# A block sum of the weights made by an accumulating DMA, for seven block pairs a layer

## The chip, the core and the metric

The kernel runs on one core of one Trainium2 chip. TensorE multiplies, VectorE (DVE) and ScalarE (ACT) work on tiles, GpSimd (POOL) does next to nothing here, and SyncE (SP) issues nearly all DMAs. The metric is the device time of one execution in microseconds; the time before is the median of three runs.

## What is computed

A decoder trunk of two layers over 512 tokens of width 1024, all in float32:

```python
def hybrid_layer(x, g_mix, w_in, sinks, w_a, w_b, w_out, g_mlp, w_up, w_down):
    h = rmsnorm(x, g_mix)
    z = h @ w_in
    ...
    ya = sliding_window_sink_attention(aq, ak, av, sinks) @ w_a
    ...
    yb = r.astype(x.dtype) @ w_b
    mixed = jax.nn.sigmoid(ga) * ya + jax.nn.sigmoid(gb) * yb
    x = x + mixed @ w_out
    h2 = rmsnorm(x, g_mlp)
    x = x + jnp.square(jax.nn.relu(h2 @ w_up)) @ w_down
    return x
```

`r` is the retention branch with its norm and gate. The change concerns the weights `w_b` (1024 by 1024), `w_out` (1024 by 1024) and `w_up` (1024 by 4096).

## The kernel before

The weights are laid out in units of 128 x 1024 numbers (512 KB) and come in the order that `unit_order` (line 58) writes down: 168 units a layer. A unit goes through three steps: a DMA loads it into a raw tile (`load_until`, line 185; three raw tiles of the pool `wpool`), ScalarE rounds it to a high part (line 255) and VectorE subtracts that from it to get the low part (line 256); then TensorE multiplies. Each product of float32 numbers is three matmuls (`products`, lines 301 to 303): high by high, high by low, low by high. There are three tiles for high and three for low parts, so the split of a unit waits until TensorE is done with the unit three before it. `split_until` (line 231) is called three units ahead of the multiplication and calls `load_until` for two more.

Some output chunks are computed two at a time as a *pair*: a 2 by 2 block product by Winograd's form of Strassen's scheme, with seven block products in place of eight. A layer has 19 pairs: for `w_b` the chunks 0 and 2, for `w_out` 2, 4 and 6, for `w_up` 4, 6 and from there each even chunk up to 30. A pair's four parts are units of their own. With `one` and `two` for the two weight rows of blocks, each with a left and a right block of 128 x 512:

- part 0: left is `one`'s left block, right is the sum of `two`'s blocks (line 221, VectorE)
- part 1: left is that sum minus `one`'s left (line 224), right is `one`'s right block
- part 2: left is `one`'s left minus `two`'s right (line 228), right is a difference out of part 1 (line 229)
- part 3: `two`'s left block

`load_part` (line 205) loads for part 0 the left block of `one` (line 210) and the whole of `two` (line 212, a raw tile of its own), and for part 1 the right block of `one` (line 215, into a tile of another pool). `add_part` (line 217) makes the sums just before the splits. `narrow_pair` (line 584) multiplies the pairs of `w_b`, `w_out` and chunk 4 of `w_up` with 256-wide matmuls; `wide_pair` (line 1250) multiplies the others with one 512-wide and one 256-wide matmul for each block (lines 1259 and 1260). Between the parts ScalarE and VectorE evacuate (lines 595 to 611 and 1286 to 1312).

Around these pairs both vector engines also have the norm's sums (lines 312, 391 to 395), the sums of input blocks for the pairs (lines 559 to 564) and the gates (lines 858, 1134, 1148), and SyncE reloads `x` (line 1181) and the gates put aside (lines 1107, 1119).

The text's order is not the order of the engines: the kernel is built with `schedule_with_timeline_sim=True` (line 1557), and a planner with durations of its own decides which of the ready instructions an engine's queue gets next. On the chip each queue then runs in that order and an instruction that has to wait holds up all behind it.

POOL has 14 instructions: constants and masks at the start, a memset in each layer's attention (line 646, the second one at 685 us) and one scaling at the end (line 531).

Of the kernel before, what the change touches and what calls it, by code (L numbers as in the profile page):

```python
# [14 lines left out]
ALU = mybir.AluOpType  # L15
# [42 lines left out]
def unit_order():  # L58

    def plain(name, *at):  # L60
        return [(name, i) for i in range(*at)]

    def pairs(src, *firsts):
        return [("pair", j, part, src) for j in firsts for part in range(4)]

    order = plain("w_in", 26) + plain("w_a", 4) + plain("w_in", 26, 46)
    order += pairs("w_b", 0, 2) + plain("w_b", 4, 8)
    order += plain("w_out", 2) + pairs("w_out", 2, 4, 6)
    for what, q, i in mlp_sequence():
        if what == "first":  # L70
            order += plain("w_up", 4)
        elif what == "pair":
            order += pairs("w_up", 8 * q + 2 * i)
        elif what == "down":
            order += plain("w_down", 8 * q + 2 * i, 8 * q + 2 * i + 2)
        else:
            order += plain("w_down", 8 * q, 8 * q + 8)
    return order
# [48 lines left out]
def decoder(ctx, tc, xT, x_first, w_in, w_a, w_b, w_out, w_up, w_down, tables, decay, band, triangles, g_last, out):  # L127
    nc = tc.nc
# [16 lines left out]
    def big(name, dtype=F32):  # L145
        return tmp.tile([P, 2, T], dtype, tag="big", name=name, bufs=7)
# [18 lines left out]
    order = [(layer, *u) for layer in range(DEPTH) for u in unit_order()]  # L165
    raws, parts, homes = {}, {}, []
# [8 lines left out]
    def raw_tile():  # L175
        return wpool.tile([P, UNIT], F32, tag="raw", name="raw")
# [8 lines left out]
    def load_until(n):  # L185
        while state["loaded"] < min(n, len(order)):
            i = state["loaded"]
            layer, name, j = order[i][:3]
            if name == "pair":
                load_part(i)  # L190
            else:
                raws[i] = raw_tile()
                for at in halves(i):
                    queue = nc.scalar if i == 0 and at.start == 0 else nc.sync
                    queue.dma_start(raws[i][:, at], weights[name][layer, j][:, at])
                    if i < 3:
                        load_x()
            state["loaded"] += 1
# [3 lines left out]

    LEFT, RIGHT = slice(0, UNIT // 2), slice(UNIT // 2, UNIT)

    def load_part(i):
        layer, _, j, part, src = order[i]
        one, two = (weights[src][layer, j + a] for a in range(2))
        if part == 0:
            raws[i] = raw_tile()
            nc.sync.dma_start(raws[i][:, LEFT], one[:, LEFT])  # L210
            raws[i + 3] = raw_tile()
            nc.sync.dma_start(raws[i + 3], two)
        elif part == 1:
            raws[i] = big("raw2").rearrange("p a t -> p (a t)")
            nc.sync.dma_start(raws[i][:, RIGHT], one[:, RIGHT])

    def add_part(i):
        part = order[i][3]
        if part == 0:
            w2 = raws[i + 3]  # L220
            nc.vector.tensor_tensor(raws[i][:, RIGHT], w2[:, RIGHT], w2[:, LEFT], ALU.add)  # L221
        elif part == 1:
            w1 = raws[i - 1]
            nc.vector.tensor_tensor(raws[i][:, LEFT], w1[:, RIGHT], w1[:, LEFT], ALU.subtract)
        elif part == 2:
            raws[i] = big("raw3").rearrange("p a t -> p (a t)")
            w1, w2, z2 = raws[i - 2], raws[i + 1], raws[i - 1]
            nc.vector.tensor_tensor(raws[i][:, LEFT], w1[:, LEFT], w2[:, RIGHT], ALU.subtract)
            nc.vector.tensor_tensor(raws[i][:, RIGHT], z2[:, RIGHT], z2[:, LEFT], ALU.subtract)

    def split_until(n):
        while state["split"] < min(n, len(order)):
            i = state["split"]
            load_until(i + 3)
            paired = order[i][1] == "pair"
            if paired:
                add_part(i)
            raw = raws[i]
            if homes and i >= len(order) - len(homes):
                home = homes[len(order) - 1 - i]  # L240
                hi, lo = (home[:, 2 * a : 2 * a + 2, :].rearrange("p a t -> p (a t)") for a in range(2))
            else:


                first = (ASIDE, ASIDE) if paired else (0, 0)
                if paired and order[i][4] == "w_up" and wide(order[i][2]):
                    first = (ASIDE, 0)
                hi, lo = (
                    wpool.tile([P, UNIT + P], F32R, tag=n, name=n)[:, a : a + UNIT] for n, a in zip(("hi", "lo"), first)
                )  # L250
            for at in (LEFT,) if paired and order[i][3] == 3 else halves(i):
                if i == 0 and at.start == 0:
                    nc.vector.tensor_copy(hi[:, at], raw[:, at])
                else:
                    nc.scalar.activation(hi[:, at], raw[:, at], AF.Copy)  # L255
                last_low[:] = [nc.vector.tensor_tensor(lo[:, at], raw[:, at], f32(hi[:, at]), ALU.subtract).ins]  # L256
            raws.pop(i - 3 if paired else i, None)
            parts[i] = (hi, lo)
            state["split"] += 1
# [1302 lines left out]
```

## Time and profile before

| | |
|---|---|
| median of three runs | 1479.97 us (1479.74 to 1479.98) |
| the profiled execution's own time | 1481.1 us |
| its span | 1478.5 us |
| units' high parts, line 255 (ScalarE) | 334 of 1.00 us mean |
| units' low parts, line 256 (VectorE) | 335 of 1.15 us mean |
| block sums of the pairs, line 221 (VectorE) | 38 of 0.69 us median |
| DMA traffic | 166.13 MB, 112 GB/s over the span |

The profile is of one execution. A matmul's duration in it is that of the whole pipeline, so that matmuls overlap: what one costs is read from the starts of two that follow each other. A row of the order of time gives start, duration, engine, line, operation, the tile written and the tiles read, shapes and, in brackets, how long the engine was idle before it and what ended that. A row that ends in "x2" stands for two. DMA issues on SyncE's queue are marked SPq.

### The profile page before, as it was taken

The numbers are of one execution on the slowest core, as the hardware profiler recorded it, in microseconds if no ns is written. First come the engines' busy times: TensorE is split into PE (matmuls) and PEld (weight loads), VectorE is DVE, ScalarE is ACT, GpSimd is POOL, SyncE is SP. The second block draws the span as 40 slices with busy tenths as digits, with TensorE's granted clock in tenths as the row PEclk, the third lists the DMA queues.
The fourth block names the chain that finished last, engine by engine and source line by source line (L and its number), as shares of the span: only waits on it lengthen the run. The fifth ranks groups of instructions, "written<-read, shape, count | busy, mean of one in ns | idle before, by whom it ended". The sixth has DMA issues, their size and how long they took to land.

```text
span 1478.5 us, 20008 instructions
## 1 busy us (share of the span) xinstructions
PE 1467.9 (99%) x7466; PEld 1249.9 (85%) x7466; DVE 1162.7 (79%) x1920; ACT 810.3 (55%) x1302; POOL 3.8 (0%) x14
## 2 busy tenths in 40 slices
PE   9999999999999999999999999999999999999998
PEld 7888888888988888888888888888889888888887
DVE  7998668778998787776678975686889977878763
ACT  7656356654674445444556743656547654444553
POOL 0000000000000000000000000000000000000000
PEclk9999999999999999999999999999999999999999
DMA  6422223246323333333543232323553323333241
GB/s 226 135 87 86 93 82 104 93 164 191 102 79 114 100 114 94 106 100 115 170 128 91 85 98 89 99 92 98 175 167 104 101 97 99 115 101 112 89 141 57
DMA packets 56945, 166.13 MB, mean 112 GB/s; under 512 B 6896, under 2 KB 7056, under 8 KB 56848
## 3 DMA queue, kind: packets, MB, share of 16 engines
q1 hardware_dynamic: 56560, 164.33, 34.9%
q8 instruction: 58, 0.95, 0.3%
q10 hardware_dynamic: 288, 0.52, 0.1%
q14 instruction: 39, 0.32, 0.1%
HBM read 153.80 MB, written 8.40 MB: 110 GB/s over the span
## 4 chain that ended last, share of the span: by engine, by line
PE 86%; DVE 6%; issue 6%; DMA 1%; ACT 0%; POOLq 0%; DVEq 0%; SPq 0%
PE mm L303 20%; PE mm L301 20%; PE mm L302 20%; PE mm L1259 10%; PE mm L1260 5%; DVE lo L256 2%; PE rv L301 2%; PE rv L302 2%; PE rv L303 2%; DVE r L309 1%; PE score L797 1%; PE r L301 1%; PE r L303 1%; PE r L302 1%; DMA inv<-row 0%
## 5 line engine op out<-in xcount | busy, mean ns | idle before, releaser
L302 PE MATMUL mm<-r,hi 128*128 128x512 f32 (+1 forms) x1568 | 572.7, 367 | 0.0
L301 PE MATMUL mm<-r,hi 128*128 128x512 f32 (+1 forms) x1568 | 570.6, 368 | 1.4 <-ACT eu L598 0.7
L303 PE MATMUL mm<-r,lo 128*128 128x512 f32 (+1 forms) x1568 | 563.1, 367 | 1.6 <-DVE lo L256 1.3
L255 ACT ACTIVATE hi<-raw 128x1024 fp32r<-128x1024 f32 (+1 forms) x334 | 334.4, 1003 | 393.1 <-PE mm L302 210.9
L256 DVE TENSOR_TENSOR lo<-raw,hi 128x512 fp32r<-128x512 f32 (+1 forms) x335 | 385.2, 1152 | 118.8 <-ACT hi L255 115.7
L303 PEld LDWEIGHTS mm<-r,lo 128*128 128x128 f32 x1568 | 293.3, 188 | 51.1 <-DVE lo L256 3.7
L301 PEld LDWEIGHTS mm<-r,hi 128*128 128x128 f32 x1568 | 294.0, 188 | 50.2 <-ACT eu L598 1.5
L302 PEld LDWEIGHTS mm<-r,hi 128*128 128x128 f32 x1568 | 294.3, 188 | 45.7
L1259 PE MATMUL mm<-r,hi 128*128 128x512 f32 x728 | 251.9, 391 | 0.0
L1260 PE MATMUL mm<-r,lo 128*128 128x256 f32 x728 | 200.4, 277 | 1.2 <-DVE lo L256 1.1
L1259 PEld LDWEIGHTS mm<-r,hi 128*128 128x128 f32 x728 | 136.5, 188 | 28.3
L1260 PEld LDWEIGHTS mm<-r,lo 128*128 128x128 f32 x728 | 136.6, 188 | 5.2 <-DVE lo L256 2.7
L1339 DVE TENSOR_TENSOR x<-x,mm 128x512 f32<-128x512 f32 x56 | 37.8, 687 | 29.2 <-PE mm L303 29.2
L1332 ACT ACTIVATE z<-z 128x512 f32<-128x512 f32 x56 | 32.5, 624 | 48.3 <-DVE z L1312 48.3
L302 PE MATMUL rv<-lo,r 128*128 128x512 f32 x128 | 49.8, 389 | 0.0
L303 PE MATMUL rv<-hi,r 128*128 128x512 f32 x128 | 49.5, 389 | 0.0
L301 PE MATMUL rv<-hi,r 128*128 128x512 f32 x128 | 49.4, 390 | 0.0
L308 ACT ACTIVATE r<-z 128x512 fp32r<-128x512 f32 x64 | 38.7, 621 | 12.6 <-DVE z L1022 12.5
L309 DVE TENSOR_TENSOR r<-z,r 128x512 fp32r<-128x512 f32 x64 | 43.1, 686 | 2.8 <-ACT r L308 2.6
L824 ACT ACTIVATE sm<-sm,st 128x256 f32<-128x256 f32 (+1 forms) x64 | 30.2, 474 | 19.1 <-DVE st L812 18.9
L1312 DVE SCALAR_TENSOR_TENSOR z<-z,rstd 128x512 f32<-128x512 f32 x52 | 35.7, 687 | 0.6
L221 DVE TENSOR_TENSOR raw<-raw 128x512 f32<-128x512 f32 x38 | 26.0, 684 | 7.0 <-DMA raw<-w_up_in 6.3
(261 smaller groups left out, 1693.0 us busy)
## 6 DMA issues: line engine op xcount, KB each, us to landing
raw<-w_in_in SPq DMA_DIRECT2D x89, 512.0 KB, 3.6
raw<-w_down_in SPq DMA_DIRECT2D x64, 512.0 KB, 3.6
raw<-w_up_in SPq DMA_DIRECT2D x36, 512.0 KB, 3.6
raw<-w_up_in SPq DMA_DIRECT2D x56, 256.0 KB, 2.8
raw<-w_b_in SPq DMA_DIRECT2D x12, 512.0 KB, 4.0
raw<-w_out_in SPq DMA_DIRECT2D x10, 512.0 KB, 7.1
raw<-w_a_in SPq DMA_DIRECT2D x8, 512.0 KB, 3.5
aside<-gb SPq DMA_DIRECT2D x8, 512.0 KB, 4.7
```

Source lines behind the costliest of these rows:

```text
L255: nc.scalar.activation(hi[:, at], raw[:, at], AF.Copy)
L256: last_low[:] = [nc.vector.tensor_tensor(lo[:, at], raw[:, at], f32(hi[:, at]), ALU.subtract).ins]
L301: nc.tensor.matmul(ps, ah, bh, start=start and i == 0, stop=False, **more)
L302: nc.tensor.matmul(ps, ah, bl, start=False, stop=False, **more)
L303: nc.tensor.matmul(ps, al, bh, start=False, stop=stop and i == n - 1, **more)
L308: nc.scalar.activation(hi, src, AF.Copy)
L309: nc.vector.tensor_tensor(lo, src, f32(hi), ALU.subtract)
L1259: nc.tensor.matmul(both, hi[:, c], m, start=start and k == 0, stop=False, **more)
L1260: nc.tensor.matmul(ps[:, :H], lo[:, c], m[:, 0, :], start=False, stop=k == 3 and start, **more)
L1312: nc.vector.scalar_tensor_tensor(z[:, :, at], z[:, :, at], 0.0, factor, ALU.max, ALU.mult)
L1332: nc.scalar.activation(z[:, i, :], z[:, i, :], AF.Square)
L1339: nc.vector.tensor_tensor(x[:, c, :], x[:, c, :], ps, ALU.add)
```

## The change

For a pair that is `summed`, that is all pairs of `w_b` and `w_out` and the chunks 4 and 6 of `w_up` (seven a layer, 14 in all), VectorE's sum at line 221 is left out. In its place SyncE loads `two`'s right block a second time, straight into the right half of part 0's tile, and a DMA issued by POOL adds `two`'s left block from HBM onto it. The other twelve pairs a layer stay as they were. `two` is still loaded whole, since parts 2 and 3 need it.

```diff
+    def summed(i):
+
+        _, _, j, _, src = order[i]
+        return src != "w_up" or j < 8
+
     def load_part(i):
...
             raws[i + 3] = raw_tile()
             nc.sync.dma_start(raws[i + 3], two)
+            if summed(i):
+                nc.sync.dma_start(raws[i][:, RIGHT], two[:, RIGHT])
+                nc.gpsimd.dma_start(raws[i][:, RIGHT], two[:, LEFT], accum_op=ALU.add)
         elif part == 1:
...
         if part == 0:
             w2 = raws[i + 3]
+            if summed(i):
+                return
             nc.vector.tensor_tensor(raws[i][:, RIGHT], w2[:, RIGHT], w2[:, LEFT], ALU.add)
```

## The prediction, made before the changed kernel ran

> **What bounds the kernel now.** I read the page first, then the busy time by stretches around the pairs that change, then TensorE's waits, then the order of time at each of these waits.
>
> ```profile
> span 1478.5 us, 20008 instructions
> PE 1467.9 (99%) x7466; PEld 1249.9 (85%) x7466; DVE 1162.7 (79%) x1920; ACT 810.3 (55%) x1302; POOL 3.8 (0%) x14
> ```
>
> TensorE is busy all but 10.6 us of the span. Whatever the change does for VectorE, it can earn only what TensorE now loses to waits, and only near the seven pairs. In the first layer these lie between 295 and 450 us:
>
> ```profile
> 345.00:360.00 15.00, 15.00 (x68) 12.43 (x67) 15.00 (x19) 7.62 (x10) 0.00 (x0) 1.00 0.74 244
> 360.00:390.00 30.00, 29.63 (x200) 27.17 (x200) 29.19 (x44) 17.67 (x27) 0.00 (x0) 1.00 0.30 91
> 390.00:410.00 20.00, 19.33 (x136) 17.85 (x136) 19.34 (x32) 14.57 (x23) 0.00 (x0) 1.00 0.39 129
> 410.00:430.00 20.00, 20.00 (x107) 17.27 (x106) 19.41 (x21) 13.41 (x17) 0.00 (x0) 1.00 0.25 79
> 460.00:600.00 140.00, 140.00 (x707) 119.02 (x706) 110.35 (x169) 67.75 (x101) 0.00 (x0) 1.00 0.33 103
> ```
>
> The columns are the stretch, its length, and the busy time of PE, PEld, DVE, ACT and POOL, then PE's clock, the DMA share and GB/s. From 345 to 430 us VectorE is busy 82.94 of 85 us: here it is a second bound beside TensorE, unlike in the long middle part (110 of 140). The clock is 1.00 everywhere. TensorE's waits of the whole kernel are few:
>
> ```profile
> PE mm L303 <- DVE lo L256: 1.3, 2, 0.7
> PE mm L1260 <- DVE lo L256: 1.1, 3, 0.5
> ...
> PE mm L301 <- ACT eu L598: 0.7, 2, 0.4
> PE mm L301 <- ACT eu L602: 0.5, 2, 0.3
> ```
>
> Apart from the warm-up's, left out here, all of them are waits for the low part of a split weight (line 256) or for an evacuation, and in each layer they stand at the pairs. This list undercounts, as a matmul's modelled end reaches over the next one's start; I therefore measure a loss from start to start. The next rows show the largest two of the first layer and the third.
>
> ```profile
> 388.29 1.06 ACT L255 ACTIVATE hi<-raw 128x1024 fp32r<-128x1024 f32 x1
> 386.24 0.69 DVE L221 TENSOR_TENSOR raw<-raw 128x512 f32<-128x512 f32 x1
> 386.84 0.74 DVE L312 SCALAR_TENSOR_TENSOR r<-x,r 128x512 fp32r<-128x512 f32 x1
> ...
> 390.91 1.22 DVE L256 TENSOR_TENSOR lo<-raw,hi 128x1024 fp32r<-128x1024 f32 x1
> 391.12 0.28 PE L301 MATMUL mm<-r,hi 128*128 128x256 f32 x1
> 391.23 0.28 PE L302 MATMUL mm<-r,hi 128*128 128x256 f32 x1
> 392.18 0.38 PE L303 MATMUL mm<-r,lo 128*128 128x256 f32 x1 [0.67 <-DVE lo L256]
> 428.87 0.63 DVE L221 TENSOR_TENSOR raw<-raw 128x512 f32<-128x512 f32 x1
> 433.88 1.22 DVE L256 TENSOR_TENSOR lo<-raw,hi 128x1024 fp32r<-128x1024 f32 x1
> 434.29 0.40 PE L1259 MATMUL mm<-r,hi 128*128 128x512 f32 x1
> 435.16 0.38 PE L1260 MATMUL mm<-r,lo 128*128 128x256 f32 x1 [0.47 <-DVE lo L256]
> 337.62 0.40 PE L302 MATMUL mm<-r,hi 128*128 128x512 f32 x1
> 338.10 0.50 PE L303 MATMUL mm<-r,lo 128*128 128x512 f32 x1
> ```
>
> A 256-wide matmul follows the one before it after 0.12 us (391.12 to 391.23). At 392.18 there lie 0.95 us between two starts, so 0.83 are lost. A 512-wide one takes twice the pitch, 0.23: at 435.16 there lie 0.87, so 0.64 are lost; at 338.10 it is 0.48, so 0.25.
>
> **The change, part by part.** *Removed:* 14 of the 38 adds of line 221, seven a layer. An add lasts 0.69 but the next instruction starts after 0.60 (386.24 to 386.84), so each frees 0.60 us of VectorE, 8.4 us in all. Most of that is not worth anything, because VectorE catches up with a late input somewhere and then waits. It counts where VectorE runs through, without idling, from an add to a split that TensorE waits for. The add at 386.24 leads to the split at 390.91 that way (the rows of that chain have no idle time behind them), so TensorE gets back 0.60 of its 0.83. The add at 428.87 leads to the split at 433.88: 0.60 of 0.64. For the first projection's second pair the following rows count:
>
> ```profile
> 325.39 0.69 DVE L221 TENSOR_TENSOR raw<-raw 128x512 f32<-128x512 f32 x1
> 326.24 1.06 ACT L255 ACTIVATE hi<-raw 128x1024 fp32r<-128x1024 f32 x1 [1.51 <-DVE raw L221]
> ```
>
> ScalarE's split idled 1.51 us for this add, and VectorE runs from there to 338; it gives the 0.25 at 338.10. So one layer earns 0.60 + 0.60 + 0.25 = 1.45. The waits listed above come in equal pairs for the two layers (two waits on line 303 of at most 0.7, together 1.3), so two layers earn 2.9. The other four adds of a layer I cost at nothing: after them VectorE waits for another engine before the next split that TensorE waits for, as in these two rows:
>
> ```profile
> 381.24 0.42 DVE L608 TENSOR_TENSOR z<-mm,eu 128x256 f32<-128x256 f32 x1 [0.38 <-PE mm L303]
> 425.60 3.36 DVE L432 RECIPROCAL rstd<-rstd 128x512 f32<-128x512 f32 x1 [0.59 <-ACT rstd L431]
> ```
>
> If I am wrong there, the two waits on ScalarE's evacuations are what could shrink (1.2 us in the list).
>
> *Added on SyncE's queue:* 14 plain loads of 256 KB, `two`'s right block straight into the sum's place. *Added on POOL's queue:* 14 accumulating loads of 256 KB. In all 7.3 MB on top of 166.13, and the question is only whether the sum has landed when ScalarE splits it.
>
> ```profile
> 304.85 0.38 SPq L210 DMA_DIRECT2D raw<-w_b_in  x1
> 318.10 0.41 SPq L215 DMA_DIRECT2D raw<-w_b_in  x1
> 321.42 0.33 SPq L212 DMA_DIRECT2D raw<-w_b_in  x1
> 349.57 0.34 SPq L210 DMA_DIRECT2D raw<-w_out_in  x1
> 376.92 0.33 SPq L210 DMA_DIRECT2D raw<-w_out_in  x1
> raw<-w_b_in SPq DMA_DIRECT2D x8, 256.0 KB, 2.6
> raw<-w_out_in SPq DMA_DIRECT2D x12, 256.0 KB, 7.3
> 360.99 1.06 ACT L255 ACTIVATE hi<-raw 128x1024 fp32r<-128x1024 f32 x1 [2.88 <-PE mm L302]
> 363.01 1.22 DVE L256 TENSOR_TENSOR lo<-raw,hi 128x1024 fp32r<-128x1024 f32 x1
> 370.86 0.28 PE L301 MATMUL mm<-r,hi 128*128 128x256 f32 x1
> ```
>
> The first three rows are one pair: its left block (line 210) is issued at 304.85, and `two` (line 212) only at 321.42, when a slot comes free. Line 215, which stands behind line 212 in the text, went ahead of it at 318.10. So the planner doesn't hold a load behind one that waits for a slot, and the new right-block load, which goes into the same tile as the left block, should go out right behind line 210, 0.4 us later. POOL's queue holds nothing else in these stretches, so what stands behind the accumulate's wait for its own load is the next accumulate alone.
>
> The trace has no accumulating DMA and none issued by POOL. From below its price is one plain load at a quiet time, 2.6 us; from above, a read and a write-back that both pass the crowded queues, twice 7.3, so 14.6 us. I take two quiet loads in series, 5.2, because outside the stretch at 345 to 360 the DMA share is 0.25 to 0.39. The time there is: from 376.92 to 388.29, 11.4 us, against 0.4 + 2.6 + 5.2 = 8.2, so the sum is 3 us early. For the pair issued at 349.57 the queues are crowded (share 0.74): 0.4 + 7.3 + 5.2 = 12.9 against 11.4 up to the split at 360.99, 1.5 us late. That split's low part ends at 364.23 and the first 256-wide matmul of the output projection comes at 370.86, so 6.6 us cover it; without this cover it would cost 1.5 a layer. Behind the late split ScalarE holds the splits of the gated sums, which have the same cover. For the pair of 304.85 the sum no longer waits for `two` at all: 21.4 us are there before 326.24, so ScalarE's 1.51 of idling goes.
>
> [...]
>
> [...]
>
> *Sum:* 1478.5 - 2.9 = 1475.6 for the span. The median of the runs, 1479.97, lies 1.5 above the span, so 1477.1 us.
>
> **Rivals.**
>
> *The sum comes late.* If the new load is issued behind line 212 after all, as it stands in the text, the pair of 321.42 has 326.24 - 321.42 = 4.8 us, against 0.4 + 2.6 + 5.2 = 8.2: 3.4 late. VectorE's low part follows ScalarE's without a gap, and TensorE runs up to it within a few tenths, so about 3 us are lost a layer there, 6 in all; the other pairs have some cover. Of the 2.9 the last 0.25 of each layer falls away, 2.4 remain: 1479.97 + 6 - 2.4 = 1483.6. It decides from a landing 4.8 us after `two` is issued. The same follows, with the load issued early, if an accumulate takes over 8.4 us (11.4 less 0.4 and 2.6). For it: the trace has no price for an accumulate. Against: the order at 318.10.
>
> [...]
>
> *Nothing moves.* The planner lays out all queues anew, and a freed 0.60 can go into another wait: TensorE stands still for the next evacuation instead. 1479.97 within 0.5 us. For it: VectorE idles nearly nowhere from 345 on, so its order is decided by due times as much as by length.
>
> *More is freed.* With the sum there early, ScalarE's splits move forward too and all waits of the list but the warm-up's vanish, counted from start to start: besides the 2.9 the rest at 392.18 (0.23) and 435.16 (0.04) and the two waits on evacuations, 1.2 in the list; with the modelled overlap of some 0.15 each about 2 us more in two layers, 1475.1 and, with the short pauses that no list shows, down to 1473.
>
> **How the numbers follow.** Forecast 0.42, late sum 0.17, port 0.06, nothing moves 0.17, more freed 0.18. What a measurement of this kernel can tell from no change is about 0.2%, 3.0 us, so the bound to faster is 1477.0 and the forecast lies on it: half of it counts as faster (0.22), half as the same (0.20). Faster is 0.22 + 0.18 = 0.40; the same 0.20 + 0.15 = 0.35; slower 0.17 + 0.06 + 0.02 = 0.25. The likeliest case's own range is 1475.3 to 1479.0. The range of all reaches from 1473.0 over the port and most of the late sums to 1485.5, as an accumulate near its upper bound costs more than the 3.4 counted.
>
> **What would show it.** Right: line 221 has 24 instructions; the new SyncE loads stand right behind line 210; ScalarE's splits of these pairs wait for no DMA; the starts at 338, 392 and 435 us and at their places in the second layer are 0.25, 0.60 and 0.60 closer to the matmul before. Wrong: ScalarE or VectorE idle at a first part of a pair with a DMA as releaser; adds beside POOL's DMAs longer than 0.69; or TensorE's total of waits stays, with other names in it.

## The result, and the profile after

The changed kernel takes 1495.38 us (median of four runs, 1494.7 to 1499.23) against 1479.89 for the kernel before on the same chip: the ratio is 1.011, with a 95% interval of 1.0093 to 1.0128. It is slower by 15.5 us, where 1477.1 was forecast; the range ended at 1485.5.

In `load_part` line 210 (`one`'s left block) has become 215, 212 (`two`) is 217 and 215 (`one`'s right block) is 223. The functions from `add_part` on stand ten lines lower: line 221 has become 231, 224 is 234, 255 and 256 are 265 and 266, 301 to 303 are 311 to 313, 598 is 608, 1259 and 1260 are 1269 and 1270. New are SyncE's load (line 219) and POOL's accumulating DMA (line 220). The head of the page of the changed kernel:

```profile
span 1493.5 us, 20063 instructions
PE 1471.5 (99%) x7466; PEld 1253.6 (84%) x7466; DVE 1154.3 (77%) x1906; ACT 809.5 (54%) x1302; POOL 16.0 (1%) x28
```

VectorE has lost its 14 adds (1920 to 1906 instructions, 8.4 us less of busy time), as the change says. TensorE's idle time is 1493.5 - 1471.5 = 22.0 us, before it was 10.6; the other 3.6 of the 15.0 us by which the span grew are busy time of TensorE, which does the same 7466 matmuls. Its four largest waits in the whole kernel, with total, count and longest:

```profile
PE mm L311 <- ACT eu L608: 6.3, 4, 2.5
PE mm L1270 <- DVE lo L266: 3.5, 2, 1.9
PE mm L311 <- ACT rstd L441: 2.7, 2, 1.3
PE mm L311 <- ACT eu L612: 1.7, 2, 0.8
```

The same two kinds stand first as before, an evacuation by ScalarE and VectorE's low part, but several times as long; the wait for the norm's square root (line 441) is new. No DMA stands in TensorE's list, so one goes a step back, to what held VectorE and ScalarE. The view of line 220's instructions says who waited for the sums, and when they landed, counted from the start of POOL's issue:

```profile
L220 POOL DMA_DIRECT2D raw<-w_out_in x6: 853/862/872, 359.1 to 1123.0; - x6
...
  DVE raw L234: 20.1, 9
  ACT hi L265: 11.2, 2
...
DMA to landing us min/median/max: 4.0/5.2/6.4
```

Line 234 is the surprise. It is part 1's subtraction, "that sum minus `one`'s left", so it reads the sum as well, and VectorE stood still for it for 20.1 us in nine places. One of them, in the order of time, on SyncE's queue, POOL, VectorE, ScalarE and TensorE (some rows left out):

```profile
379.90 0.33 SPq L215 DMA_DIRECT2D raw<-w_out_in  x1
380.28 0.42 SPq L219 DMA_DIRECT2D raw<-w_out_in  x1
384.44 0.86 POOL L220 DMA_DIRECT2D raw<-w_out_in  x1 [16.67 <-DVE z L618]
```

```profile
384.45 0.68 DVE L239 TENSOR_TENSOR raw<-raw 128x512 f32<-128x512 f32 x1
385.66 1.22 DVE L266 TENSOR_TENSOR lo<-raw,hi 128x1024 fp32r<-128x1024 f32 x1
390.27 0.69 DVE L234 TENSOR_TENSOR raw<-raw 128x512 f32<-128x512 f32 x1 [3.40 <-DMA raw<-w_out_in]
390.88 0.41 DVE L1209 TENSOR_TENSOR x<-x,mm 128x256 f32<-128x256 f32 x1
```

```profile
391.33 0.72 ACT L321 ACTIVATE r<-x 128x512 fp32r<-128x512 f32 x1 [2.84 <-DVE x L1209]
392.48 0.36 ACT L608 ACTIVATE eu<-mm 128x256 f32<-128x256 f32 x1
393.00 1.05 ACT L265 ACTIVATE hi<-raw 128x1024 fp32r<-128x1024 f32 x1
```

```profile
390.15 0.28 PE L313 MATMUL mm<-r,lo 128*128 128x256 f32 x1
392.89 0.58 PE L311 MATMUL mm<-r,hi 128*128 128x256 f32 x1 [2.46 <-ACT eu L608]
393.27 0.41 PE L312 MATMUL mm<-r,hi 128*128 128x256 f32 x1
393.48 0.41 PE L311 MATMUL mm<-r,hi 128*128 128x256 f32 x1
```

Read it from the end. TensorE stops from 390.15 to 392.89 for an evacuation (line 608). ScalarE could not do that one, since work ahead of it on its queue waited 2.84 us for an update of `x` (line 1209). VectorE had not made the update, as the subtraction of line 234 stood ahead of it and waited 3.40 us. The subtraction waited for the accumulate, which POOL issued at 384.44; it landed 5.8 us later. POOL's row names line 618 as what it waited for, but that one had ended at 383.93. The load of 380.28 landed after 3.5 us, and at each of the four places where the view has the load's landing, POOL's issue follows it by 0.5 to 0.7 us; so the load is the likelier releaser. ScalarE's own split of the sum comes only at 393.00, without any wait for a DMA. Its queue had been held up by VectorE's stop itself, so this row doesn't tell whether the sum was in time for ScalarE; the third experiment does.

In the trace of before the subtraction stood further back, as line 224:

```profile
384.52 0.41 DVE L1199 TENSOR_TENSOR x<-x,mm 128x256 f32<-128x256 f32 x1
...
388.71 0.69 DVE L224 TENSOR_TENSOR raw<-raw 128x512 f32<-128x512 f32 x1
```

Between these two came a low part, the add of 386.24, lines 312 and 395 and another low part. The planner has taken the subtraction to the front of them, directly behind a low part of the pair before: ahead of line 1199 (now 1209) and of the four that are left when the add is gone.

The matmuls after the stop are 0.21 us apart (393.27 to 393.48) and not 0.12. The stretches around it, with the granted clock behind the five busy times:

```profile
389.00:392.50 3.50, 1.43 (x13) 1.22 (x11) 2.23 (x5) 1.17 (x3) 0.00 (x0) 1.00 0.09 16
392.50:396.00 3.50, 3.11 (x14) 3.11 (x15) 3.50 (x7) 1.56 (x4) 0.00 (x0) 0.53 0.14 37
396.00:400.00 4.00, 4.00 (x36) 4.00 (x34) 4.00 (x7) 1.43 (x2) 0.00 (x0) 0.98 0.49 152
```

For about 3.4 us the clock is at half (0.53 in the middle row, which has a little of full clock in it; in slices of half a us it is 0.74, then 0.50 from 393.0 to 396.0, then 0.85): some 1.7 us of work more are lost. One other such stretch lies in the second layer, from 1181 us on (0.50 from 1181.5 to 1184.5), also behind a stop of over 2 us. Together that is 3.4 us, nearly all of the 3.6 by which TensorE's busy time grew. In the trace of before there is no such stretch between 10 and 1470 us: the granted clock is 1.00 there in every 20 us, where the two that hold the half clock here have 0.91.

By the starts of the same matmuls, after minus before, the shift grows from 0.8 at the first pair of `w_b` to 5.2 at the third of `w_out` and 7.3 at the first matmul of `w_down`, and the second layer does the same again, to 14.7. The first 0.8 is there from the span's first 10 us on (the same matmul starts at 9.24 and at 8.46) and has nothing to do with the pairs; all the rest arises at the pairs that changed.

### The profile page after: what moved, and what is told of

Same layout as the page of the kernel before. It is cut to its first block, busy times and chain, and to the rows that moved or that the text cites. A ratio compares the mean times of both kernels' runs of the same rounds, so it can differ in the third digit from the quotient of the medians.

```text
span 1493.5 us, 20063 instructions
## 1 busy us (share of the span) xinstructions
PE 1471.5 (99%) x7466; PEld 1253.6 (84%) x7466; DVE 1154.3 (77%) x1906; ACT 809.5 (54%) x1302; POOL 16.0 (1%) x28
## 3 DMA queue, kind: packets, MB, share of 16 engines
q0 software_dynamic: 2016, 3.67, 1.6%
## 5 line engine op out<-in xcount | busy, mean ns | idle before, releaser
L234 DVE TENSOR_TENSOR raw<-raw 128x512 f32<-128x512 f32 x38 | 26.1, 688 | 20.2 <-DMA raw<-w_out_in 12.1
```

## The experiments

Four explanations were to be told apart: that the sums land late (called A in the expectations; A1 is that it acts through VectorE's subtraction, A2 through the split); that the order which the planner made anew costs by itself (B); that the new DMAs, or POOL's issuing of them, disturb the others (C); and later, that the relief is there but given back at the norm's square root (D; E is that the relief is worth nothing). All but POOL's adds at the end are edits of the changed kernel. Each was run beside the kernel before, whose median lay between 1479.73 and 1480.03.

**No accumulating DMA** (the sum then lacks `two`'s left block).

```diff
-                nc.gpsimd.dma_start(raws[i][:, RIGHT], two[:, LEFT], accum_op=ALU.add)
+                pass
```

> The accumulating DMA is left out, so that the sum is the second row's right block alone; VectorE's add stays away and SyncE's extra load stays. Theory A (the sum lands later than the planner's order allows, and VectorE and ScalarE stand in front of it): with the accumulate gone no VectorE or ScalarE instruction waits for a part-0 tile any more, and the time falls back to 1476 to 1481 us. Theory B (the order that the planner lays out without the add is bad in itself, whatever the landing): 1488 us or more. Theory C (3.67 MB more of plain loads crowd the queues): half of the loss stays, 1485 to 1490.

Measured: 1479.2 us, ratio 0.9995 (0.9986 to 1.0005). So the whole loss hangs on the accumulate; the second load from SyncE and the missing adds cost nothing together. But they also earn next to nothing: the 0.8 us by which this kernel is ahead can't be told from none by the interval. TensorE's waits in this kernel:

```profile
PE mm L311 <- ACT rstd L441: 2.7, 2, 1.3
PE mm L311 <- ACT eu L612: 1.6, 2, 0.8
...
PE mm L1270 <- DVE lo L266: 0.4, 2, 0.2
```

The waits for low parts that the forecast counted on (2.4 in all) are down to 0.4, as they should be. In their place stand new ones, at line 612 (0.5 before, now 1.6) and at the norm's square root (none before, now 2.7). Here is the latter in the order of time, on ScalarE and TensorE:

```profile
424.30 1.06 ACT L265 ACTIVATE hi<-raw 128x1024 fp32r<-128x1024 f32 x1 [3.67 <-PE mm L312]
425.38 1.28 ACT L441 ACT_TABLE_LOAD   x1
426.68 0.69 ACT L441 ACTIVATE rstd<-ssq,x 128x512 f32<-128x512 f32 x1
```

```profile
427.42 0.39 PE L311 MATMUL mm<-r,hi 128*128 128x256 f32 x1 [1.33 <-ACT rstd L441]
```

The split at 424.30 is part 2's of `w_up`'s chunk 4. In the trace of before it stood behind the square root:

```profile
424.88 0.69 ACT L431 ACTIVATE rstd<-ssq,x 128x512 f32<-128x512 f32 x1 [1.35 <-PE ssq L430]
```

Now the planner takes the split first. It waits 3.67 us for TensorE, the table load of 1.28 us comes only behind it, and the square root starts at 426.68, 1.8 us later than before. TensorE's start is 1.5 us ahead of before at the first matmul of `w_up`'s chunk 4 (0.4 of it since the first 10 us), and by the first of chunk 6 it is 0.3 behind: 1.8 are lost in between. The relief itself is there. By TensorE's starts 0.2 us are gained at 338, 0.6 at 378 and 0.9 at 392; some 0.75 are lost at 325, behind the evacuation of line 612.

**A plain DMA by POOL in the place of the accumulating one** (the sum is then a plain copy).

```diff
-                nc.gpsimd.dma_start(raws[i][:, RIGHT], two[:, LEFT], accum_op=ALU.add)
+                nc.gpsimd.dma_start(raws[i][:, RIGHT], two[:, LEFT])
```

> POOL's DMA only copies the left block over the right one, it does not add; the order of all engines is that of the changed kernel. Theory A, if what is late is the chain of two loads and POOL's issue: landing about 5 us after POOL's issue as with the add (5.2 us there), and 1493 to 1497 us. If the adding itself is what takes long (reading the destination): landing at 3 us or less, and 1480 to 1488 us.

Measured: 1482.54 us, ratio 1.0018 (1.0008 to 1.0027). All engines' orders of instructions are the same as in the changed kernel: the planner makes no difference between an accumulating DMA and a plain one. The chip does. The view of line 220's instructions:

```profile
L220 POOL DMA_DIRECT2D raw<-w_out_in x6: 536/537/538, 358.3 to 1114.8; - x6
...
  ACT hi L265: 9.5, 2
  DVE raw L234: 8.7, 7
...
DMA to landing us min/median/max: 2.9/3.7/5.3
```

The sum lands 1.5 us earlier after the start of POOL's issue (3.7 against 5.2); 0.33 of that is the issue itself (0.54 against 0.86). VectorE's waits fall from 20.1 to 8.7, and the time by 12.8 us. So with the same order, queues and traffic from HBM, the accumulate's own length is worth 12.8 of the 15.5 us, give or take some 2: this kernel's ten runs reach from 1480.7 to 1485.61. At the place shown above VectorE waits 0.78 instead of 3.40, and there is no stretch of half clock (mean granted clock 0.999, against 0.997 in the changed kernel):

```profile
385.52 0.69 DVE L234 TENSOR_TENSOR raw<-raw 128x512 f32<-128x512 f32 x1 [0.78 <-DMA raw<-w_out_in]
```

**Part 1's subtraction doesn't read the sum** (its result is then zero); the accumulates stay.

```diff
-            nc.vector.tensor_tensor(raws[i][:, LEFT], w1[:, RIGHT], w1[:, LEFT], ALU.subtract)
+            nc.vector.tensor_tensor(raws[i][:, LEFT], w1[:, LEFT] if summed(i) else w1[:, RIGHT], w1[:, LEFT], ALU.subtract)
```

> Line 234 of a summed pair subtracts the left block from itself, so that it no longer reads the sum; the accumulates stay, and only the split (ScalarE, line 265) waits for them. Theory A1 (VectorE's wait at line 234 is what costs): no VectorE wait for a part-0 DMA, ScalarE's 11 us in two places stay, and 1480 to 1485 us. Theory A2 (the wait only moves: the split's high part and with it VectorE's low part stand there in its place): 1489 us or more.

Measured: 1482.5 us, ratio 1.0017 (1.0008 to 1.0027); 12.9 us of the changed kernel's time are gone, though the sums land as late as there (5.2 us median). The waits of ScalarE for the sum stay:

```profile
ACT hi L265 <- DMA raw<-w_out_in: 11.9, 2, 6.1
```

At the place shown above the split, with nothing in its way, comes at 390.56 and doesn't wait for the accumulate, which POOL issued at 384.78 and which landed 5.3 us later, at 390.1:

```profile
390.56 1.05 ACT L265 ACTIVATE hi<-raw 128x1024 fp32r<-128x1024 f32 x1
```

So there the sum was in time for ScalarE, by half a us, and late for VectorE. TensorE's remaining waits are on evacuations and the square root:

```profile
PE mm L311 <- ACT eu L608: 2.7, 3, 1.2
PE mm L311 <- ACT rstd L441: 2.7, 2, 1.3
PE mm L311 <- ACT eu L612: 1.7, 2, 0.8
```

This tells the readers apart: 11.9 us of ScalarE's idling at the first pairs of `w_out` cost little, and nearly all of the loss goes with the 20.1 us of VectorE's. It also speaks against a disturbance by the DMAs or by POOL, since all of them are still there. What it can't tell is which of the other waits make the 3.3 us by which it and the plain copy stand above the kernel without a second step. The planner's order around the subtraction differs a little too.

**The subtraction held later**, behind the low part of part 0.

```diff
-            nc.vector.tensor_tensor(raws[i][:, LEFT], w1[:, RIGHT], w1[:, LEFT], ALU.subtract)
+            with tc.issue_after(last_low[0]) if summed(i) else ExitStack(): nc.vector.tensor_tensor(raws[i][:, LEFT], w1[:, RIGHT], w1[:, LEFT], ALU.subtract)
```

> Line 234's subtraction of a summed pair is put behind the low part of part 0 on VectorE. Theory A: VectorE's waits for DMAs at line 234 (20.1 us in 9 places) go; the late split of the output projection's first pair (ScalarE, 11.2 us in two places) stays, with its cover: 1480 to 1486 us. Theory B: the rest of the order is as new as before, 1490 us or more.

Measured: 1486.05 us, ratio 1.0041 (1.0026 to 1.0056), a hair above the range that was expected. VectorE doesn't wait for the sum any more, and 9.3 us come back, but now it is ScalarE that waits for the subtraction, as its queue shows:

```profile
389.40 1.06 ACT L265 ACTIVATE hi<-raw 128x1024 fp32r<-128x1024 f32 x1
392.70 1.06 ACT L265 ACTIVATE hi<-raw 128x1024 fp32r<-128x1024 f32 x1 [2.24 <-DVE raw L234]
```

The hold is too late here. Between the early place and this one there may be a better one; none was tried.

**A later landing**: POOL copies the block plainly first and accumulates after it (the sum is then twice the left block).

```diff
-                nc.gpsimd.dma_start(raws[i][:, RIGHT], two[:, LEFT], accum_op=ALU.add)
+                for more in ({}, dict(accum_op=ALU.add)): nc.gpsimd.dma_start(raws[i][:, RIGHT], two[:, LEFT], **more)
```

> POOL first copies the left block and then adds it, so that every sum lands about 4 us later (3.7 from issue to landing, with the plain copy). Theory A: each of the fourteen pairs now costs about what it is late, and more where TensorE pauses so long that the clock is halved: 1515 to 1550 us. Theory B (the order): 1493 to 1500 us.

Measured: 1507.13 us, ratio 1.0186 (1.0171 to 1.0202), 11.8 above the changed kernel and below the range expected for A and above the one for B. By the view of line 220's instructions ScalarE waits 28.3 us for the sums and VectorE 26.1, which is only 6.0 more than in the changed kernel. The planner knows of the extra DMA, though not of its length, and puts the subtraction later; so a third step isn't paid in full, and the kernel isn't the clean doubling it was meant to be. There are four stretches of half clock here (mean granted clock 0.995).

**One kind of pair at a time.** Three kernels, each with one line changed: only `w_b`, only `w_out`, only `w_up`'s chunks 4 and 6.

```diff
-        return src != "w_up" or j < 8
+        return src == "w_b"
```

> Only the four pairs of w_b are summed by the DMA; the ten of w_out and w_up have VectorE's add as before. Theory A: those sums have 12 to 21 us from the first load to their split and no VectorE instruction waited for them in the changed kernel, so 1478 to 1481 us. Theory B or C: each pair costs its share, four of fourteen, so about 1484 us.

```diff
-        return src != "w_up" or j < 8
+        return src == "w_out"
```

> Only the six pairs of w_out are summed by the DMA. Theory A: these carry 12.1 of VectorE's 20.1 us and all of ScalarE's 11.2 us of waiting for sums, and one half-clock stretch of 3.4 us: 1485 to 1490 us.

```diff
-        return src != "w_up" or j < 8
+        return src == "w_up" and j < 8
```

> Only the four pairs of w_up are summed by the DMA. Theory A: 8.0 of VectorE's 20.1 us of waiting lie here, and the wait for the norm's factor on ScalarE that the new order brings: 1483 to 1488 us. If the pairs cost independently, the three subsets (w_b +2.3, w_out, w_up) add up to about +15 us.

Measured: 1482.35 us, ratio 1.0019 (1.0009 to 1.0028), for `w_b`; 1487.37, 1.0055 (1.004 to 1.007), for `w_out`; 1486.91, 1.0047 (1.0032 to 1.0062), for `w_up`. Against their kernels before that is 2.3, 7.6 and 7.1 us, together 17.0, a little more than the whole. The last two came as expected in time. The kernel with `w_out` has two stretches of half clock, at 392 and 1126 us (mean granted clock 0.996), where one was expected, and the one with `w_up` has none (0.999), though in the changed kernel the second lies at a pair of `w_up` (the stop before 1181.16 is on line 1270). `w_b` was a miss: its sums are in time, no engine waits for them, and still it loses 2.3. Two of TensorE's waits in that kernel:

```profile
PE mm L311 <- ACT eu L612: 1.7, 2, 0.8
PE mm L311 <- DVE gb L868: 1.1, 1, 1.1
```

The others are those of before. The first was 0.5 there and the second, for a gate, is new: 2.3 together. They come with the order laid out anew; which move in it makes them was not tried.

**The square root first again**, without the accumulate: the split that had overtaken it is held behind it.

```diff
-                    nc.scalar.activation(hi[:, at], raw[:, at], AF.Copy)
+                    with tc.issue_after(last_sqrt[0]) if order[i][2:] == (4, 2, "w_up") else ExitStack(): nc.scalar.activation(hi[:, at], raw[:, at], AF.Copy)
```

> As noacc (the sum lacks the left block, nothing waits for POOL), and ScalarE's split of part 2 of w_up's pair 4 is held behind the norm's square root, where it stood before the change. Theory D (the relief of VectorE is worth its 1.5 us a layer, and the new order gives it back by putting a split that waits for TensorE ahead of the square root): TensorE's wait for line 441 (2.7 us) goes, 1475.5 to 1477.5 us. Theory E (the relief is worth nothing in any order): 1478.5 us or more.

Measured: 1484.4 us, ratio 1.0031 (1.0019 to 1.0042); 4.7 us slower than the kernel before, where D had 1475.5 to 1477.5. The time lies in E's range, but one order can't show that the relief is worth nothing in any. The wait for the square root is gone, but the hold moved what comes behind it, and TensorE's waits for low parts have come back at the next pairs:

```profile
PE mm L1270 <- DVE lo L266: 2.7, 2, 1.3
PE mm L313 <- DVE lo L266: 2.4, 4, 1.0
```

**POOL adds instead of VectorE**, from the row that is loaded anyway; no DMA is added. It computes the same sums as before.

```diff
-            nc.vector.tensor_tensor(raws[i][:, RIGHT], w2[:, RIGHT], w2[:, LEFT], ALU.add)
+            (nc.gpsimd if summed(i) else nc.vector).tensor_tensor(raws[i][:, RIGHT], w2[:, RIGHT], w2[:, LEFT], ALU.add)
```

> No DMA is added: POOL makes the fourteen sums out of the loaded row, as VectorE did. Theory A (lateness against the order decides, not who adds): the sum is late only by what POOL takes longer than VectorE's 0.69 us; if that is under 2 us, 1477 to 1481 us. If POOL and VectorE hold each other up at their reads, VectorE's two-input instructions beside it get longer than 0.69 and the time is 1483 us or more.

Measured: 1490.93 us, ratio 1.0074 (1.006 to 1.0088), a miss for A. The view of POOL's adds (min/median/max in ns), the longest of them, and the waits for them of VectorE and ScalarE:

```profile
L226 POOL TENSOR_TENSOR raw<-raw x14: 1297/1666/3755, 302.6 to 1164.3; 128x512 f32<-128x512 f32 x14
```

```profile
359.49 3.75 POOL L226 TENSOR_TENSOR raw<-raw 128x512 f32<-128x512 f32 x1 [33.29 <-DMA raw<-w_out_in]
```

```profile
DVE raw L229 <- POOL raw L226: 14.3, 12, 1.2
```

```profile
ACT hi L260 <- POOL raw L226: 18.5, 8, 4.4
```

The time lies where the other expectation put it, but VectorE's instructions beside the longest of POOL's adds got no longer: the four of 128 x 512 that start between 359.61 and 361.41 take 0.68 each. With no DMA behind the sum, the same subtraction (line 229 in this kernel) waits again, for a sum that comes about 1.2 us late in twelve places. With the square root held first as above, this kernel takes 1490.91 (1.0077, 1.0063 to 1.0091), no better:

> POOL's adds together with the split held behind the square root. Theory D with a sum that lands in time: 1475.5 to 1478 us, faster than both kernels. If POOL's adds are slow or hold VectorE up: no better than 1480.

None of these kernels clearly beats the one before; the best, without the accumulate, equals it within the interval and doesn't make the sum.

## Why the prediction was wrong

**The step that failed** is the deadline. "The time there is: from 376.92 to 388.29, 11.4 us, against 0.4 + 2.6 + 5.2 = 8.2, so the sum is 3 us early": this looked at ScalarE's split alone. Line 224 reads the sum too, and nothing held it at 388.71. The planner, which treats the accumulate like a plain copy, set it ahead of five others, and on the chip VectorE was ready for it at 386.9 and got its operand at 390.27. The kernel whose subtraction doesn't read the sum shows the price, 12.9 of 15.5 us; the plain copy shows the same from the other side, 12.8. At its old place, 388.71 - 376.92 = 11.8 us behind the left block's issue, the subtraction would still have found the sum: so the prediction lacked both the second reader and that the planner would move it. It had itself said that VectorE is a second bound there (busy 82.94 of 85 us), but drew from it only that freed time is worth something, not that a stop on VectorE costs most of its length (here 12.9 of 20.1 us).

**The accumulate's price** held by luck: 5.2 us taken, 5.2 median measured (4.0 to 6.4), but not as two loads of 2.6 in series. A plain copy from POOL's queue lands after 3.7, and accumulating adds 1.5. The rest of the sum was undersized. At the place shown the load took 3.5 where 2.6 was taken, the 0.7 from its landing to POOL's issue was left out, and the accumulate took 5.8: from the left block's issue to the subtraction's start 390.27 - 379.90 = 10.4 us, not 8.2. Against ScalarE's split this alone would still have been in time, by the 0.5 us that the kernel without the subtraction's reading shows, and not by 3.

**The place of the new load** held: right behind the left block's, 0.38 us later.

**The cover at the first pair of `w_out`** held as a mechanism. The sum was not 1.5 but about 3.1 us late there: the split starts at 365.67 instead of 360.99, and 1.6 of these 4.7 us the whole kernel was behind by then. ScalarE idles 6.01 us where it had idled 2.88. TensorE's starts show 0.6 of it by 380.

**The relief** of 1.45 a layer, 2.9 in all, was oversized. The low parts' waits did go, and the starts at 338 and 392 gained 0.2 and 0.9 where 0.25 and 0.60 were forecast. But the kernel without the accumulate kept 0.8 at most, because the new order gives it back at the square root and at line 612. "The other four adds cost at nothing" failed the same way: `w_b` alone loses 2.3 us without a single late sum. Whether another order would keep the 2.9 is open; the one attempt lost more elsewhere.

**The rivals.** That the sum comes late had the right event, but its conditions (a load behind line 212, or an accumulate over 8.4 us) were both not met, its reader was ScalarE, and its price of 6 us was less than half. That POOL's work holds VectorE up, which the chances and the range count under the name port (0.06), no run shows: VectorE's instructions at 384.45 and 385.05, beside POOL's issue from 384.44 to 385.30, took 0.68 each, and VectorE's busy time fell by the full 8.4 us. "Nothing moves" is what the change would have been with a sum in time (1479.2). Of the range's upper end, no case had a wait on VectorE in it. The prediction's list of what would show it wrong did name the sign: "ScalarE or VectorE idle at a first part of a pair with a DMA as releaser"; for ScalarE it came so (6.01 us at 365.67), for VectorE at a second part, and that was the costly one.

**The account**, by medians: the adds gone and the order laid out anew -0.8; the sum in two steps through POOL, if its DMA were a plain one, +3.3 (1482.54 - 1479.2); the accumulate's extra 1.5 us a sum +12.8 (1495.38 - 1482.54), in which are the two stretches of half clock with about 3.4. What the 3.3 is made of stays open.

## What to carry to other kernels

When a result is made by another engine or queue, list every instruction that reads it and take the earliest that the engine's order may reach, not the first that looks urgent; on VectorE, which took its queue in order and ran through without idling, most of the late operands' delay was lost (12.9 of 20.1 us here), as all that stood behind them was late as well. Where a planner orders the queues, ask whether it knows the length of the new operation: 1.5 us more for each of 14 DMAs, which its order took no account of, cost 12.8 us here. And don't count on a few tenths of relief on such an engine until the order that follows from them has been seen.

## What the runs showed of the hardware

An accumulating DMA of 256 KB from HBM into SBUF takes POOL 0.86 us to issue and lands 5.2 us after the start of the issue (4.0 to 6.4), a plain one from the same queue 0.54 and 3.7 (2.9 to 5.3).

Two stops of TensorE, of 2.62 us up to 392.89 and of 2.08 us up to 1181.16, had a stretch of about 3.4 us at half clock behind them (granted clock 0.50). A third, of 2.56 us up to 1131.08, had none (1.00 from 1131 to 1135). What decides between them, these runs don't show.

POOL's add took between 1.30 and 3.75 us for the same shape, 1.67 in the median, where VectorE's took 0.69 in the same kernel. In the longest, from 359.49 on, VectorE's instructions beside it took 0.68 each. What made POOL's long was not shown.
